# Moving the low weights of a split-precision decoder block by 128 bytes in their buffers

## The chip, the cores and the metric

The kernel runs on one core of a Trainium2 chip. Its time is the device time of one execution in microseconds. Before the change it is 522.29 us, the median of 3 runs (522.06 to 523.15). Five engines work side by side, each through its own list of instructions: TensorE (PE, with its weight loads shown apart as PEld), VectorE (DVE), ScalarE (ACT), GpSimd (POOL) and SyncE (SP), whose queue issues nearly all transfers.

## The reference, cut to what matters

One decoder block of width 1024 over 256 tokens: a normalised input, three token mixers side by side (a sparse attention, an mLSTM and attention to a fixed memory), gated and merged, then a SwiGLU channel mixer.

```python
h = rmsnorm(x, g_pre_mix);  z = h @ w_in            # queries, keys, gates, ...
y = gm0 * (y_nsa @ w_proj_nsa) + gm1 * (y_ml @ w_proj_ml) + gm2 * (y_mem @ w_proj_mem)
x = x + rmsnorm(y @ w_out, g_post_mix)
gate, up = rmsnorm(x, g_pre_ffn) @ w_ffn_in          # 1024 x 5632
x = x + rmsnorm((silu(gate) * up) @ w_ffn_down, g_post_ffn)
```

All is float32, and nearly all of the work is matrix products with weights that are read once.

## The kernel before, in words

**Split precision.** TensorE takes float32 in a rounded form ("float32r") at one pass. To keep the precision, each operand is split in two: a high part, the operand rounded by a copy on ScalarE, and a low part, the operand less its high part, by a subtraction on VectorE (`split`, lines 970 to 973). A product of two operands then takes three matmuls (`mm3`, line 1005): high weights with high input, high weights with low input, low weights with high input. This document calls these three a triplet.

**Units.** Weights come in 161 units of 128 x 1024 numbers (512 KB), each by one transfer into one of four `raw` buffers (`fetch`, line 979). From there the split writes `whi` and `wlo`, of which there are four buffers each (`room` at line 990, `parts` at 995, `unit` at 1000). A buffer of these two is 1088 numbers wide, 64 more than a unit, so that a unit can stand further in. Where it stands is the argument `shift`, counted in numbers of 4 bytes, one for the high and one for the low part.

**Two ways to use a unit.** In `fmaj` (line 1010, called through `fpair`, line 1018, and in the projections at line 1696) the weights are held in TensorE, 128 x 128 at a time, and 256 columns of input (the 256 tokens) stream past them. A unit is 8 such blocks, so 8 triplets, 24 matmuls with 24 weight loads; the high block is loaded for each of its two matmuls. These calls take the default shift. In `tmaj` (line 1025) and in the class `Blocks` (line 1054) it is the other way round: activations are held and 512 columns of weights stream. These calls pass their own shift, 48 or 0. The memory's keys (line 1192) use `room()` with the default shift and hold weights over 256 columns too. The four first units of the FFN's gate and up rows are written into buffers of their own (`wq`, line 1775), which the default does not reach.

**Addresses.** `lay_out` (line 880) gives each buffer a fixed place. A table (`RESIDUE`, line 877) sets at which remainder of 256 bytes it begins. `whi`, `wlo`, `raw` and the buffers tagged G, C, V and qs begin at 0; those tagged KK, E, Y and hh, among them the inputs of `fmaj`, begin at 192. A `whi` or `wlo` buffer is 4352 bytes long, 17 times 256, so all four begin at remainder 0, and each block of 128 columns (512 bytes) does as well. The weights of the gates (`gw`, line 1292) stand 32 numbers, 128 bytes, into a `whi` buffer. A shift of 48 numbers is 192 bytes.

**Order.** Every operation is first recorded (`Plan.record`, line 196) and then issued by a planner (`schedule`, line 369) from modelled costs, due times and a written table of corrections (`EARLY`, line 547). Costs depend on engine, kind and size of an operation, not on addresses. All instructions are issued by the planner at line 917, which is therefore the line of every row in the profile; rows are told apart by the names of tiles. `hh` is the normalised input of the mixers, `xc` that of the FFN, `u` the FFN's hidden values; `pd`, `pss`, `pt` and `pv` are tiles of the accumulator.

**Stages** (us from the span's start): the memory's keys and values and the input projections up to about 270, with attention and mLSTM among them; the three output projections to 308; the output product to about 322; the first part of the FFN input, with products saved by sums of row blocks, to 360; the rest of the FFN input, `block` by `block` (line 1804, 2 units each), to 453; the FFN's down product to the end.

Of the kernel before, what the change touches and what calls it, by code (L numbers as in the profile page):

```python
# [920 lines left out]
def block_kernel(ctx, tc, order, xN, xT, memN, head, cst, vec, row, wg, w1, w2, W, out):  # L921
# [48 lines left out]
    def split(hi, lo, src):  # L970
        op = ACT.activation(hi, src, AF.Copy)
        DVE.tensor_sub(lo, src, hi.bitcast(F32))
        return op
# [5 lines left out]
    def fetch(key):  # L979
        if key in ahead:  # L980
            if not room4:
                room4.append(bigt("KK", 1, [P, len(ahead), 1024], F32, "rawx"))
            raw = ready[key] = room4[0][:, ahead.index(key), :]
        else:
            raw = ready[key] = wpool.tile([P, 1024], F32, tag="raw", bufs=4, name="raw")
        dma(out=raw, in_=W[len(order)])
        order.append(key)
        return raw

    def room(shift=(0, 0)):  # L990


        return [wpool.tile([P, 1088], F32R, tag=t, bufs=4, name=t)[:, n:n + 1024] for t, n in zip(("whi", "wlo"), shift)]

    def parts(raw, into=None, shift=(0, 0)):
        hi, lo = into or room(shift)
        split(hi, lo, raw)
        return hi, lo

    def unit(key, into=None, shift=(0, 0)):  # L1000
        if key not in ready:
            fetch(key)
        return parts(ready.pop(key), into, shift)
# [14 lines left out]
    def fpair(xs, w, i, ps_new=ps_d):  # L1018

        ps = ps_new([P, 2, S])  # L1020
        for j in range(2):
            fmaj(ps[:, j, :], xs, range(KD), unit((w, 2 * i + j)))
        return ps

    def tmaj(xs, *key, n=4, ps_new=ps_d, into=None, last=0, shift=lambda u: 48):


        ps = [ps_new([P, 512]) for _ in range(2)]

        def use(u, tb, wu):  # L1030
            hi, lo = wu
            for kk in range(2):
                k = 2 * u + kk
                t = slice(tb * P, (tb + 1) * P)
                w = slice(kk * 512, (kk + 1) * 512)
                PE.matmul(ps[tb], xs[0][:, k, t], hi[:, w], start=(k == 0), stop=False)
                PE.matmul(ps[tb], xs[0][:, k, t], lo[:, w], start=False, stop=False)
                PE.matmul(ps[tb], xs[1][:, k, t], hi[:, w], start=False, stop=(k == 2 * n - 1))

        for u in range(n - last):  # L1040
            w = unit((*key, u), shift=(shift(u),) * 2)
            for tb in range(2):
                use(u, tb, w)
        us = range(n - last, n)
        ws = [unit((*key, u), into and into[u], (shift(u),) * 2) for u in us]
        for tb in range(2):
            for u, w in zip(us, ws):
                use(u, tb, w)
        return ps
# [4 lines left out]
    class Blocks:  # L1054
# [30 lines left out]
        def seven(self, n, u):  # L1085

            k, first, last = 2 * u, n == 0, n == len(self.sums) - 1
            both = self.both.pop(u, None) or self.pair(u)
            raw, dif = self.shift(u), (48, 48)
            s = [[self.sums[n][:, x, i] for x in range(2)] for i in range(4)]  # L1090
            w0 = parts(both[:, 0].rearrange("p k n -> p (k n)"), shift=raw)
            w1 = room(dif)
            split(w1[0][:, H1], w1[1][:, H1], both[:, 1, 1])
            self.three(self.m1, self.held(k, 0), w0, H0, first, last)
            self.into(0, 0, self.held(k + 1, 0), w0, H1)
            self.into(1, 0, s[3], w1, H1)
            t = work.tile([P, 1024], F32, tag="p", bufs=2, name="dif")
            DVE.tensor_sub(t.rearrange("p (k n) -> p k n", k=2), both[:, 1], both[:, :, 0])
            w = parts(t, shift=dif)
            self.three(self.m5, s[0], w, H0, first, last)  # L1100
            self.three(self.m7, s[2], w, H1, first, last)
            t2 = work.tile([P, 1024], F32, tag="p", bufs=2, name="dif")
            DVE.tensor_add(t2[:, H0], t[:, H1], both[:, 0, 0])
            DVE.tensor_sub(t2[:, H1], both[:, 0, 1], t2[:, H0])
            w = parts(t2, shift=raw)
            self.three(self.m6, s[1], w, H0, first, last)
            self.into(0, 1, self.held(k + 1, 1), w, H1)
# [84 lines left out]
    for u in range(4):  # L1192
        if u and ("mem_k", u) not in ready:
            fetch(("mem_k", u))
        raw = ready.pop(("mem_k", u)) if u else mt[:, 264:1288]
        w = room()
        pieces = HEAD[u]
        for h in range(2):
            if h < pieces:
                c = slice(1024 // pieces * h, 1024 // pieces * (h + 1))  # L1200
                split(w[0][:, c], w[1][:, c], raw[:, c])
            mem_in(2 * u + h)
        for k in (2 * u, 2 * u + 1):
            b = lambda j: slice(512 * (k % 2) + P * j, 512 * (k % 2) + P * j + P)
            for i, (x, y) in enumerate(((w[0], mh), (w[0], ml), (w[1], mh))):
                for j in range(4):
                    PE.matmul(kps[j // 2][:, j % 2, :], x[:, b(j)], y[:, k, :],
                              start=k == 0 and i == 0 and j % 2 == 0, stop=k == KD - 1 and i == 2 and j % 2 == 1,
                              skip_group_check=True)
# [806 lines left out]
```

## Time and profile before

| what | before |
|---|---|
| median of 3 runs | 522.29 us |
| the profiled execution | 523.74 us |
| its span, first to last instruction | 521.7 us |
| granted TensorE clock, mean | 0.996 |
| TensorE busy | 513.6 us, 98% of the span, 3778 matmuls |
| its weight loads | 484.7 us, 93% |
| VectorE / ScalarE busy | 435.1 us (83%) / 360.0 us (69%) |
| GpSimd busy | 6.8 us (1%) |
| DMA | 97.18 MB, mean 186 GB/s |

The profile is that of one execution. A row of a group names line, engine, operation, `out<-in` by the program's tiles, sizes, the count, the busy time in us, the mean length of one in ns, and the idle time before them with what ended it. Matmuls overlap: the length of one is longer than the step from one start to the next, and it is the step that counts for the time. A row of a stretch gives its length, then for each engine the busy time and in brackets the number of instructions that touch it (TensorE, its weight loads, VectorE, ScalarE, GpSimd), then the granted clock, the DMA share and GB/s. A row of the timeline gives the start in us, the length in us, and how many instructions of one kind were merged in it.

### The profile page before, as it was taken

To read this page: it belongs to the slowest core of one execution; us is meant where nothing else is said; L and a number is where in the kernel's file an instruction comes from. 1 tells how busy PE (TensorE), PEld (TensorE's weight loads), DVE (VectorE), ACT (ScalarE), POOL (GpSimd) and SP (SyncE) were. 2 spreads that over 40 slices of the span, in tenths; PEclk is the share of its full clock that TensorE was granted. 3 is DMA by queue.
4 is the path that set the end of the run, shared out by engine and by line. 5 is a ranking of instruction groups with operands and counts; after the bars stand their busy time and mean duration, and the time that the engine had idled before them with its cause. 6 is when DMAs were issued, how large, how long until landed. Compare 5 with 4: busy or idle time off the path is not lost.

```text
span 521.7 us, 10043 instructions
## 1 busy us (share of the span) xinstructions
PE 513.6 (98%) x3778; PEld 484.7 (93%) x3778; DVE 435.1 (83%) x902; ACT 360.0 (69%) x723; POOL 6.8 (1%) x20
## 2 busy tenths in 40 slices
PE   8999999999999999999999999999999999999995
PEld 8899998989899999999999998888999999988884
DVE  5699898798989998987888868789976568798983
ACT  6787897577799887977996437748454456566641
POOL 0000000000000100000000000100000000000000
PEclk9999999999999999999999999999999999999998
DMA  8987547635343273254485653734656555463422
GB/s 310 394 340 272 183 148 210 208 122 201 122 146 138 86 279 122 82 202 162 165 296 198 232 173 131 281 144 163 228 174 202 171 193 171 154 215 108 138 106 80
DMA packets 28560, 97.18 MB, mean 186 GB/s; under 512 B 3296, under 2 KB 5216, under 8 KB 28256
## 3 DMA queue, kind: packets, MB, share of 16 engines
q1 hardware_dynamic: 28368, 96.29, 53.4%
q8 instruction: 29, 0.48, 0.4%
q10 hardware_dynamic: 144, 0.26, 0.1%
q14 instruction: 19, 0.16, 0.1%
HBM read 94.44 MB, written 1.05 MB: 183 GB/s over the span
## 4 chain that ended last, share of the span: by engine, by line
PE 94%; DMA 3%; DVE 1%; ACT 1%; SPq 0%; issue 0%; DVEq 0%
PE pd L917 51%; PE pss L917 28%; PE pvn L917 3%; PE pt L917 2%; PE sc L917 2%; PE ptn L917 2%; DMA xt<-in_xT 2%; DMA raw<-in_W 1%; PE pv L917 1%; DVE wlo L917 1%; PE ph L917 1%; PE ptx L917 1%; PE psm L917 1%; PE pvm L917 1%; PE pn L917 0%; PE pq L917 0%
## 5 line engine op out<-in xcount | busy, mean ns | idle before, releaser
L917 ACT ACTIVATE whi<-raw 128x1024 fp32r<-128x1024 f32 (+1 forms) x146 | 151.6, 1050 | 78.8 <-PE pd L917 39.1
L917 DVE TENSOR_TENSOR wlo<-raw,whi 128x1024 fp32r<-128x1024 f32 (+1 forms) x146 | 174.3, 1205 | 31.3 <-ACT whi L917 28.7
L917 PE MATMUL pd<-hh,whi 128*128 128x256 f32 x800 | 147.0, 280 | 0.0
L917 PEld LDWEIGHTS pd<-hh,whi 128*128 128x128 f32 x800 | 123.6, 188 | 0.2
L917 PE MATMUL pd<-hh,wlo 128*128 128x256 f32 x400 | 111.8, 280 | 0.0
L917 PEld LDWEIGHTS pd<-hh,wlo 128*128 128x128 f32 x400 | 75.3, 188 | 0.1
L917 PE MATMUL pss<-xc,whi 128*128 128x256 f32 x384 | 70.0, 281 | 0.0
L917 PEld LDWEIGHTS pss<-xc,whi 128*128 128x128 f32 x384 | 59.7, 189 | 0.6
L917 PE MATMUL pss<-xc,wlo 128*128 128x256 f32 x192 | 52.9, 281 | 0.0
L917 PEld LDWEIGHTS pss<-xc,wlo 128*128 128x128 f32 x192 | 35.9, 189 | 0.3
L917 PE MATMUL pd<-xc,whi 128*128 128x256 f32 x192 | 35.2, 282 | 0.0
L917 DVE CUSTOM_DVE_ANT_0 sc<-sc,msk 128x16 f32<-128x16 f32 (+2 forms) x96 | 27.2, 313 | 6.0 <-PE sc L917 3.8
L917 PE MATMUL pd<-whi,hh 128*128 128x512 f32 x96 | 31.6, 397 | 0.0
L917 PEld LDWEIGHTS pd<-xc,whi 128*128 128x128 f32 x192 | 29.7, 189 | 0.0
L917 ACT ACTIVATE pp<-sc,mx 128x128 f32<-128x128 f32 (+1 forms) x64 | 26.8, 432 | 0.5 <-DVE mx L917 0.4
L917 PE MATMUL pd<-xc,wlo 128*128 128x256 f32 x96 | 26.6, 281 | 0.0
L917 PE MATMUL pd<-whi,u 128*128 128x512 f32 x72 | 24.1, 392 | 0.0
L917 ACT ACTIVATE whi<-dif 128x1024 fp32r<-128x1024 f32 x12 | 12.6, 1056 | 13.3 <-PE pd L917 7.4
L917 PEld LDWEIGHTS pd<-whi,hh 128*128 128x128 f32 x96 | 17.9, 188 | 3.2
L917 PE MATMUL pd<-wlo,hh 128*128 128x512 f32 x48 | 19.0, 396 | 0.0
L917 DVE TENSOR_TENSOR wlo<-dif,whi 128x1024 fp32r<-128x1024 f32 x12 | 14.6, 1223 | 5.2 <-ACT whi L917 5.1
L917 PE MATMUL pss<-whi,u 128*128 128x512 f32 x56 | 18.7, 390 | 0.0
(392 smaller groups left out, 1134.1 us busy)
## 6 DMA issues: line engine op xcount, KB each, us to landing
raw<-in_W SPq DMA_DIRECT2D x145, 512.0 KB, 4.1
raws<-in_W SPq DMA_DIRECT2D x12, 512.0 KB, 4.6
w<-in_w SPq DMA_DIRECT2D x2, 1024.0 KB, 7.8
rawx<-in_W SPq DMA_DIRECT2D x4, 512.0 KB, 5.5
xn<-in_xN SPq DMA_DIRECT2D x2, 512.0 KB, 9.8
mn<-in_memN SPq DMA_DIRECT2D x2, 512.0 KB, 7.5
xt<-in_xT SPq DMA_DIRECT2D x2, 512.0 KB, 8.4
kk<-kk SPq DMA_DIRECT2D x8, 128.0 KB, 3.1
```

The lines of the kernel that those rows point to most:

```text
L917: op.ins_ = getattr(op.real, op.method)(*map(arg, op.a), **{k: arg(x) for k, x in op.kw.items()})
```

## The change

The default of `shift` goes from (0, 0) to (0, 32) in `room`, `parts` and `unit`. Where no shift is passed, the low part of a unit therefore begins 32 numbers, 128 bytes, further in its buffer, at remainder 128 of 256 bytes instead of 0. The high part stays at 0. VectorE writes the low part there and TensorE loads it from there. Calls that pass a shift, and units written into buffers of their own, are untouched. Instructions, their order and their waits stay the same.

```diff
-    def room(shift=(0, 0)):
+    def room(shift=(0, 32)):
         return [wpool.tile([P, 1088], F32R, tag=t, bufs=4, name=t)[:, n:n + 1024] for t, n in zip(("whi", "wlo"), shift)]
 
-    def parts(raw, into=None, shift=(0, 0)):
+    def parts(raw, into=None, shift=(0, 32)):
         hi, lo = into or room(shift)
         split(hi, lo, raw)
         return hi, lo
 
-    def unit(key, into=None, shift=(0, 0)):
+    def unit(key, into=None, shift=(0, 32)):
         if key not in ready:
             fetch(key)
         return parts(ready.pop(key), into, shift)
```

## The prediction

> **What bounds the kernel now.** I read the page first, then the waits of TensorE, then stretches of time side by side, and last the timeline where a pace changes. The page, with its matmul groups:
>
> ```profile
> PE 513.6 (98%) x3778; PEld 484.7 (93%) x3778; DVE 435.1 (83%) x902; ACT 360.0 (69%) x723; POOL 6.8 (1%) x20
> ...
> PE 94%; DMA 3%; DVE 1%; ACT 1%; SPq 0%; issue 0%; DVEq 0%
> ...
> L917 PE MATMUL pd<-hh,whi 128*128 128x256 f32 x800 | 147.0, 280 | 0.0
> ...
> L917 PE MATMUL pd<-hh,wlo 128*128 128x256 f32 x400 | 111.8, 280 | 0.0
> ...
> L917 PE MATMUL pss<-xc,whi 128*128 128x256 f32 x384 | 70.0, 281 | 0.0
> ...
> L917 PE MATMUL pss<-xc,wlo 128*128 128x256 f32 x192 | 52.9, 281 | 0.0
> ...
> L917 PE MATMUL pd<-xc,whi 128*128 128x256 f32 x192 | 35.2, 282 | 0.0
> ...
> L917 PE MATMUL pd<-xc,wlo 128*128 128x256 f32 x96 | 26.6, 281 | 0.0
> ```
>
> TensorE is busy for 98% of the span and makes 94% of the chain. These six groups (2064 matmuls) are most of those that hold weights for 256 columns. The waits of TensorE, all of them:
>
> ```profile
> PE warm L917 <- POOL mhalf L917: 1.0, 1, 1.0
> PE pd L917 <- ACT whi L917: 0.7, 1, 0.7
> ```
>
> So after the start TensorE waits for nobody. Its time can change only through the pace at which matmuls follow each other. That pace is not one number. Seven stretches that hold little but matmuls over 256 columns; the first count in brackets is the number of matmuls that touch the stretch:
>
> ```profile
> 36.00:40.00 4.00, 4.00 (x36) 4.00 (x35) 3.93 (x9) 3.92 (x8) 0.00 (x0) 1.00 1.02 410
> 44.00:48.00 4.00, 4.00 (x38) 4.00 (x37) 3.91 (x9) 2.85 (x5) 0.00 (x0) 1.00 1.03 411
> 193.00:198.00 5.00, 5.00 (x45) 5.00 (x44) 4.19 (x11) 4.43 (x12) 0.00 (x0) 1.00 0.31 106
> 222.00:229.00 7.00, 7.00 (x64) 7.00 (x63) 6.57 (x17) 4.71 (x12) 0.00 (x0) 1.00 0.65 219
> 272.00:302.00 30.00, 30.00 (x267) 30.00 (x267) 25.18 (x31) 18.13 (x21) 0.00 (x0) 1.00 0.64 226
> 377.00:407.00 30.00, 30.00 (x257) 30.00 (x256) 19.78 (x28) 13.73 (x21) 0.00 (x0) 1.00 0.58 191
> 407.00:437.00 30.00, 30.00 (x257) 30.00 (x256) 20.99 (x35) 16.50 (x24) 0.00 (x0) 1.00 0.51 172
> ```
>
> and one group from the fifth and one from the sixth stretch:
>
> ```profile
> L917 PE MATMUL pss<-ynh,wlo 128*128 128x256 f32 x32 | 8.8, 276 | 0.0
> ```
> ```profile
> L917 PE MATMUL pss<-xc,wlo 128*128 128x256 f32 x43 | 11.7, 281 | 0.0
> ```
>
> A matmul touches a stretch if it starts in it or up to its own length before it, so the step is (stretch + length) / count: (30 + 0.276)/267 = 113.4 ns in the projections and (30 + 0.281)/257 = 117.8 ns in the FFN input. Same shape, same granted clock of 1.00: a quick and a slow pace, 4.4 ns apart. Traffic does not explain it: 36 to 40 us (118.9 ns) and 44 to 48 us (112.5 ns) move the same 410 GB/s with DVE equally full. The timeline shows where it turns:
>
> ```profile
> 374.00 0.28 PE L917 MATMUL pd<-xc,wlo 128*128 128x256 f32 x1
> ...
> 374.34 0.28 PE L917 MATMUL pd<-xc,wlo 128*128 128x256 f32 x1
> ...
> 374.68 0.28 PE L917 MATMUL pd<-xc,wlo 128*128 128x256 f32 x1
> ...
> 374.91 0.60 PE L917 MATMUL ptu<-cs,ut 128*128 128x128 f32 x4
> ...
> 375.46 0.28 PE L917 MATMUL pd<-xc,wlo 128*128 128x256 f32 x1
> ...
> 375.82 0.28 PE L917 MATMUL pd<-xc,wlo 128*128 128x256 f32 x1
> ...
> 376.17 0.28 PE L917 MATMUL pd<-xc,wlo 128*128 128x256 f32 x1
> ```
>
> A triplet (high weights with high input, high with low, low with high) takes 0.34 us before four transposes and 0.353 us after them (0.71 for two), and from there the slow pace holds to 437 us at least. So the pace is a state: something foreign to the run sets it, and an unbroken run keeps it. I read it as two regular streams of reads, input and next weights, which either mesh or keep bumping into each other; the profile shows the two paces, not their cause.
>
> **The change part by part.** No instruction, wait, transfer or queue position is added, removed or moved, and the planner's costs do not look at addresses. What moves is the start of `wlo` in its buffer: 128 bytes on, for the units taken with the default shift. By the code these are 108 units of 24 matmuls (mem_k 4, kv 8, qk_ml 8, q_mem 4, q_nsa 8, g_merge 24, projections 16, ffn_in 36): 2592 matmuls, a third of which (864) load low weights.
>
> *DVE's write of the low part.* The nearest rows are the same subtraction written to places 0 and 192 past a multiple of 256 bytes (400 to 440 us, 308 to 318 us):
>
> ```profile
> L917 DVE TENSOR_TENSOR wlo<-raw,whi 128x1024 fp32r<-128x1024 f32 x14 | 17.0, 1224 | 12.6 <-ACT whi L917 12.6
> ```
> ```profile
> L917 DVE TENSOR_TENSOR wlo<-raw,whi 128x1024 fp32r<-128x1024 f32 x3 | 3.7, 1221 | 0.1
> ```
>
> Three ns apart, and TensorE does not wait for DVE: nothing either way. Were that cover gone, 3 ns on 108 writes would be 0.3 us. ACT writes the high part where it did.
>
> *The load of low weights beside the stream of the low input.* The input starts 192 past a multiple of 256 bytes, all weights at 0; now every third load starts at 128, and the next goes back to 0. No row shows just this. Two come near. First, the compressor's two chains of 16 (input at 0, stationary at 192, the same distance as 192 and 128):
>
> ```profile
> 52.26 2.05 PE L917 MATMUL ph<-w1s,st 128*128 128x256 f32 x16
> 54.14 0.41 PE L917 MATMUL pd<-hh,whi 128*128 128x256 f32 x2
> ```
> ```profile
> 56.99 1.98 PE L917 MATMUL ph<-w1s,st 128*128 128x256 f32 x16
> 58.81 0.33 PE L917 MATMUL phT<-w2t,hs 128*128 128x64 f32 x2
> ```
>
> 1.88/16 = 117.5 ns and 1.82/16 = 113.8 ns: the new distance, held throughout, also has both paces. So the distance alone sets nothing; what is new is that it jumps twice in each triplet. Second, the gates' weights, which stand at 128 while the same input streams at 192, over 512 columns, against the quiet end of the kernel:
>
> ```profile
> 40.96 0.86 PE L917 MATMUL pgf<-hh,gw 128*128 128x512 f32 x3
> 41.67 0.28 PE L917 MATMUL pd<-hh,whi 128*128 128x256 f32 x1
> ...
> 41.90 1.32 PE L917 MATMUL pgf<-hh,gw 128*128 128x512 f32 x5
> 43.06 0.40 PE L917 MATMUL pd<-hh,whi 128*128 128x256 f32 x2
> ```
> ```profile
> 498.53 0.39 PE L917 MATMUL pd<-wlo,u 128*128 128x512 f32 x1
> ...
> 499.21 0.39 PE L917 MATMUL pd<-wlo,u 128*128 128x512 f32 x1
> ```
>
> 0.71/3 = 237 and 1.16/5 = 232 ns against 0.68/3 = 226.7: 5 to 10 ns more. But the stretch before them was at the slow pace (36 to 40 us) and the stretch behind them at the quick one (44 to 48 us): the jump of distance went with a change to the quick pace. From these rows a low load lies between -4.4 ns, with its two neighbours gaining as much, and +10 ns.
>
> I take the gain as likeliest: a slow pace lives on regular repetition, and a jump twice per triplet breaks it within a few steps, while a state in which reads miss each other is less in need of it. The stock of slow steps: in the FFN input some 800 of 864 at 4.4 ns, 3.5 us (its groups' means are 281 to 282 ns, a fast stretch like the one before 374.9 us is the exception); in the projections' 384 nearly none (272 to 302 us); in the remaining 1344 about half by the four short stretches (two slow, two fast), 3.0 us, with bounds 0 and 5.9. Together 6.5 us. Other work still cuts in, each cut is a new entry, and a slow pace needs some steps to break, so I take two thirds: **-4.3 us**. On the profiled execution, 523.74 us with its span of 521.70, that gives 519.4. The median of the runs is 1.45 us lower, 518.0 on its base. If that 1.45 us is itself slow stock (the run of 272 to 302 us alone, 265 steps, would be worth 1.2 us if it were slow), the median's stock is 5.05, two thirds are 3.4, and 518.9 results. I forecast **518.4 us**. Room for it is there: at 407 to 437 us DVE is at 70%, ACT at 55% and DMA at 51%, and a pace 4% quicker leaves all under 75%; what is late next is nothing.
>
> **Rivals.** *The low load collides (slower).* Loading low weights at 128 while the low input streams costs more than it now does, in each triplet, as at the gates' weights. For it: their 5 to 10 ns, in all eight. Against it: few samples, a longer stream, and a quick pace behind them. With 864 low loads at 5 to 10 ns, less the 4.4 that about half already pay, it is 2.6 to 6.7 us slower; with a middle of 4, **526.3 us**. It decides when a low load adds over 5 ns while the rest turns fast (4.3/864), or over 1.2 ns while the rest stays (1.04/864).
>
> *The entries are only drawn anew.* Both states survive the jumps, but each run enters at another phase. The run from 375 to 437 us and on may turn fast (62/0.1178 = 526 steps or more, -2.3 us), the one from 272 to 302 us slow (265 steps, +1.2), and the early ones cancel. For it: four transposes are enough to turn a run. It gives 520.0 to 523.5, and half way to the first **521.2 us**.
>
> *The address does nothing.* The pace is set at entry by something that does not see where weights lie; the two compressor chains, one distance and two paces, speak for it. Then **522.3 us**. The Trainium skill, "TensorE: Matmul & The Clock Gate", Part 2 ("Step-by-step: what each phase is for"), says that TensorE has two independent read ports into SBUF, so that loading the next weights takes nothing from the running matmul; by that rule the sum is zero and this rival holds. The trace does not refute it, but two paces at clock 1.00 without a wait are nothing it foresees.
>
> **How the numbers follow.** Forecast 0.48; collision 0.22; entries drawn anew 0.18; nothing 0.12. What a measurement can tell from no change is 0.2%, 1.04 us: faster is below 521.25. The forecast lies there wholly, and of the redraw, whose middle stands at that edge, 0.10; the redraw gives 0.05 to the same and 0.03 to slower. Faster 0.48 + 0.10 = 0.58; same 0.12 + 0.05 = 0.17; slower 0.22 + 0.03 = 0.25. The forecast's own range is 516.2 (all 6.5 less a few entries, off the median) to 520.6 (a quarter of the stock). The range reaches into the collision to its middle, 516.2 to 526.0.
>
> **What would show it.** Right: stretches of pure FFN input hold about 267 matmuls in 30 us instead of 257, with 276 ns each instead of 281, and the run behind the transposes at 375 us is fast or turns fast within a few triplets. Collision: triplets of over 0.353 us, the third step the long one. Redraw: long runs of both paces, in other places. Nothing: the same stretches, the same counts. Counts unchanged and time lower, or a new wait on TensorE, would make my account wrong.

## The result, and the profile after

The changed kernel takes 519.25 us (median of 5 runs, 517.58 to 519.31) against 523.03 us of the kernel before in the same session (5 runs, 522.06 to 523.56): a ratio of 0.9925 with a 95% interval of 0.9906 to 0.9944, 3.8 us less. The profiled execution took 519.27 us with a span of 516.7, against 523.74 and 521.7: 4.5 us less in time, 5.0 in span. The forecast was 518.4 us, and -4.3 us on the profiled execution. In what follows, one of the 12 executions of the kernel with both operands moved took 1840.86 us and is left out of its ratio.

The page of the kernel after, its engines, the chain by engine and the six groups of matmuls over 256 columns:

```profile
PE 508.7 (98%) x3778; PEld 479.9 (93%) x3778; DVE 434.8 (84%) x902; ACT 360.2 (70%) x723; POOL 6.8 (1%) x20
...
PE 94%; DMA 3%; DVE 1%; ACT 1%; SPq 0%; issue 0%; DVEq 0%
...
L917 DVE TENSOR_TENSOR wlo<-raw,whi 128x1024 fp32r<-128x1024 f32 (+1 forms) x146 | 174.4, 1206 | 29.3 <-ACT whi L917 28.1
L917 PE MATMUL pd<-hh,whi 128*128 128x256 f32 x800 | 146.2, 279 | 0.0
...
L917 PE MATMUL pd<-hh,wlo 128*128 128x256 f32 x400 | 111.4, 279 | 0.0
...
L917 PE MATMUL pss<-xc,whi 128*128 128x256 f32 x384 | 67.9, 276 | 0.0
...
L917 PE MATMUL pss<-xc,wlo 128*128 128x256 f32 x192 | 52.1, 276 | 0.0
...
L917 PE MATMUL pd<-xc,whi 128*128 128x256 f32 x192 | 34.1, 277 | 0.0
...
L917 PE MATMUL pd<-xc,wlo 128*128 128x256 f32 x96 | 26.1, 276 | 0.0
```

The shares are nearly the same, the counts the same. TensorE's busy time went from 513.6 to 508.7 us, which is nearly the whole difference of the spans. The four groups that read the FFN input `xc` went from 281 and 282 ns to 276 and 277, the two that read `hh` only from 280 to 279. All waits of TensorE in the kernel after:

```profile
PE warm L917 <- POOL mhalf L917: 1.0, 1, 1.0
PE pd L917 <- ACT whi L917: 0.4, 1, 0.4
PE pss L917 <- DVE wlo L917: 0.3, 2, 0.2
```

1.7 us in all, as before. The seven stretches of the prediction, in the kernel after:

```profile
36.00:40.00 4.00, 4.00 (x38) 4.00 (x37) 3.93 (x8) 3.93 (x7) 0.00 (x0) 1.00 1.04 417
44.00:48.00 4.00, 4.00 (x38) 4.00 (x37) 3.91 (x9) 2.32 (x4) 0.00 (x0) 1.00 1.02 409
193.00:198.00 5.00, 5.00 (x46) 5.00 (x45) 4.24 (x12) 4.62 (x12) 0.00 (x0) 1.00 0.38 111
222.00:229.00 7.00, 7.00 (x64) 7.00 (x63) 6.11 (x18) 4.41 (x11) 0.00 (x0) 1.00 0.61 205
272.00:302.00 30.00, 30.00 (x267) 30.00 (x267) 25.72 (x32) 17.61 (x20) 0.00 (x0) 1.00 0.61 213
377.00:407.00 30.00, 30.00 (x268) 30.00 (x266) 19.66 (x28) 14.63 (x21) 0.00 (x0) 1.00 0.53 176
407.00:437.00 30.00, 30.00 (x267) 30.00 (x266) 23.15 (x42) 17.01 (x27) 0.00 (x0) 1.00 0.61 202
```

Both long stretches of the FFN input hold 267 or 268 matmuls instead of 257. By the prediction's own arithmetic a step there takes (30 + 0.276)/267 = 113.4 ns instead of 117.8. The projections (272 to 302 us) were at 267 and stayed there. The timeline of the kernel after at the four transposes that had turned the pace (they start at 372.88 us here, at 374.91 before):

```profile
372.88 0.60 PE L917 MATMUL ptu<-cs,ut 128*128 128x128 f32 x4
...
373.44 0.28 PE L917 MATMUL pd<-xc,wlo 128*128 128x256 f32 x1
...
373.79 0.28 PE L917 MATMUL pd<-xc,wlo 128*128 128x256 f32 x1
...
374.13 0.28 PE L917 MATMUL pd<-xc,wlo 128*128 128x256 f32 x1
...
374.47 0.28 PE L917 MATMUL pd<-xc,wlo 128*128 128x256 f32 x1
```

From low load to low load 0.35, 0.34 and 0.34 us: the first triplet after the transposes is slow, the next are quick. Before the change the same place led into over 60 us at the slow pace.

The packed traces hold the start of every matmul, so the steps can also be read one by one: from the start of a matmul that holds weights over 256 columns to the start of the next, if that is one too. Steps over 135 ns, which are interruptions, are left out. Before the change nearly all of these steps lie near 113 or near 118 ns; those of 116 ns or more are counted here as slow. A run is a series of such steps without another instruction or an interruption between them; there are 102. "The rest" are the memory's keys and values and the input projections.

| steps of 116 ns or more | before | after |
|---|---|---|
| FFN input | 791 of 845 | 28 of 845 |
| output projections | 47 of 371 | 9 of 371 |
| the rest | 527 of 1223 | 235 of 1220 |
| among the first twelve of each run | 395 of 808 | 271 of 808 |
| among all later ones | 970 of 1631 | 1 of 1628 |

The last two rows show what the change does. A run can still start at the slow pace after an interruption, but from its thirteenth step on it is quick, in every stage. The kernels with part of the change, below, agree: with the FFN input alone moved, 0 of its 747 later steps are slow, and with everything else moved 0 of 580 in the rest.

### The profile page after: what moved, and what is told of

Same layout as the page of the kernel before. It is cut to its first block, busy times and chain, and to the rows that moved or that the text cites. A ratio compares the mean times of both kernels' runs of the same rounds, so it can differ in the third digit from the quotient of the medians.

```text
span 516.7 us, 10043 instructions
## 1 busy us (share of the span) xinstructions
PE 508.7 (98%) x3778; PEld 479.9 (93%) x3778; DVE 434.8 (84%) x902; ACT 360.2 (70%) x723; POOL 6.8 (1%) x20
## 4 chain that ended last, share of the span: by engine, by line
PE 94%; DMA 3%; DVE 1%; ACT 1%; SPq 0%; issue 0%; DVEq 0%
PE pd L917 51%; PE pss L917 28%; PE pvn L917 3%; PE pt L917 2%; PE sc L917 2%; PE ptn L917 2%; DMA xt<-in_xT 2%; DMA raw<-in_W 1%; PE pv L917 1%; DVE wlo L917 1%; PE ph L917 1%; PE ptx L917 1%; PE psm L917 1%; PE pvm L917 1%; PE pq L917 1%; PE pn L917 0%
## 5 line engine op out<-in xcount | busy, mean ns | idle before, releaser
L917 ACT ACTIVATE whi<-raw 128x1024 fp32r<-128x1024 f32 (+1 forms) x146 | 151.6, 1050 | 74.6 <-PE pd L917 36.3
L917 DVE TENSOR_TENSOR wlo<-raw,whi 128x1024 fp32r<-128x1024 f32 (+1 forms) x146 | 174.4, 1206 | 29.3 <-ACT whi L917 28.1
L917 PE MATMUL pss<-xc,whi 128*128 128x256 f32 x384 | 67.9, 276 | 0.0
L917 PE MATMUL pd<-xc,whi 128*128 128x256 f32 x192 | 34.1, 277 | 0.0
```

What stands on the lines that cost most here:

```text
L917: op.ins_ = getattr(op.real, op.method)(*map(arg, op.a), **{k: arg(x) for k, x in op.kw.items()})
```

## The experiments

All of them are moves of addresses, and in the traces the order of instructions on each engine is the changed kernel's in each. The diffs are against the kernel before unless they say otherwise, and each ratio is to the kernel before as it ran beside (medians of 522.62 to 523.09 us). "Counts" are the matmuls in 272 to 302, 377 to 407 and 407 to 437 us (where a fence has no row for the last, it is as in the one before it): 267 or 268 is the quick pace, 256 to 258 a mean step like that of the slow pace. Before: 267, 257, 257. After: 267, 268, 267.

### Both parts moved: place without a jump

```diff
-    def room(shift=(0, 0)):        # and parts, unit
+    def room(shift=(32, 32)):
```

> High and low weights both stand 128 bytes in; nothing jumps within a triplet. Theory J (the jump of remainder between the loads of a triplet breaks the slow pace): the slow pace can live again, so long stretches at 117.8 ns come back; if the FFN input is entered as before, 30 us of it from 377 us hold about 257 matmuls and the time is 522 to 523.5 us; 267 matmuls there would need another entry. Rival P (the place 128 of the low weights is itself better than 0): no slow stretches, 267 matmuls, 519 us. Rival R (any new addresses only draw the entries anew): some stretches of each pace, 519 to 523.5 us.

Measured: 525.27 us, ratio 1.0046 (1.0034 to 1.0058).

```profile
272.00:302.00 30.00, 30.00 (x267) 30.00 (x267) 24.89 (x31) 18.39 (x23) 0.00 (x0) 1.00 0.63 226
377.00:407.00 30.00, 30.00 (x257) 30.00 (x256) 20.56 (x30) 13.78 (x20) 0.00 (x0) 1.00 0.55 183
407.00:437.00 30.00, 30.00 (x257) 30.00 (x256) 20.16 (x35) 15.74 (x23) 0.00 (x0) 1.00 0.51 171
```

All weights now stand where only the low ones stand in the changed kernel, and the long runs are what they were before: one quick, two slow. So the place 128 has no merit of its own for them; the low weights have to stand apart from the high ones. Most of its 2.7 us are lost in the early stages: in the rest, 988 of 1225 steps are slow, against 527 of 1223 before, which is 2.0 us. A stretch that was quick before (first row) has become slow (second row, with both parts moved):

```profile
43.50:48.00 4.50, 4.50 (x42) 4.50 (x41) 4.41 (x10) 3.34 (x6) 0.00 (x0) 1.00 1.02 394
```
```profile
43.50:48.00 4.50, 4.50 (x40) 4.50 (x39) 4.41 (x10) 2.48 (x5) 0.00 (x0) 1.00 0.98 394
```

### The low part 256 bytes further

```diff
-    def room(shift=(0, 0)):        # and parts, unit
+    def room(shift=(0, 64)):
```

> Low weights stand 256 bytes in, remainder 0 again, but at another address. Theory J with a period of 256 bytes: as the kernel before, long slow stretches, 257 matmuls in 30 us of FFN input, 522 to 523.5 us. Rival P2 (distance between the high and the low part counts, whatever the remainder) : 267 matmuls, 519 us. Rival R: some stretches of each pace, not the same ones as before.

Measured: 522.36 us, ratio 1.0003 (0.9992 to 1.0013).

```profile
272.00:302.00 30.00, 30.00 (x267) 30.00 (x266) 25.72 (x32) 17.57 (x20) 0.00 (x0) 1.00 0.60 209
377.00:407.00 30.00, 30.00 (x257) 30.00 (x256) 18.77 (x27) 13.90 (x20) 0.00 (x0) 1.00 0.56 181
```

Twice the move and no effect: for the low weights it is the remainder of 256 bytes that counts, as far as one such move can show it. The long runs also have their old paces, which speaks against entries that are drawn anew by any touch.

### The low part 64, 192 or 96 bytes further

```diff
-    def room(shift=(0, 0)):        # and parts, unit
+    def room(shift=(0, 16)):       # 64 bytes; (0, 48): 192; (0, 24): 96
```

> Low weights stand 64 bytes in: a jump of half the size. Theory J: any jump breaks the slow pace, 267 matmuls in 30 us of FFN input, 518 to 520 us. Rival P (place 128): slow stretches stay, 257 matmuls, 522 to 523.5 us. If only half a period of 256 bytes works, this stands with the kernel before or between.

> Low weights stand 192 bytes in, the remainder of the input itself: a jump of 64 bytes the other way. Theory J: 267 matmuls in 30 us of FFN input, 518 to 520 us. Rival P (place 128): slow stretches stay, 257 matmuls, 522 to 523.5 us. Rival C (weights at the remainder of the input they are loaded beside collide): over 117.8 ns per step, slower than 523.5 us.

> As the change, but the low weights stand 96 bytes further instead of 128, between the 64 that kept only the slow pace (528.5 us, 256 matmuls in 377 to 407 us) and the 128 of the change. If only the half period itself does it: 528 us and 256 or 257. If a jump near the half is enough: 519.2 us and 267. Between: both paces possible, 521 to 524 us.

Measured: 528.52 us with 64 bytes, ratio 1.0111 (1.0098 to 1.0124); 527.92 us with 192, ratio 1.0103 (1.0089 to 1.0118); 527.67 us with 96, ratio 1.0095 (1.0078 to 1.0111). With 64 bytes:

```profile
272.00:302.00 30.00, 30.00 (x256) 30.00 (x255) 24.18 (x31) 19.03 (x25) 0.00 (x0) 1.00 0.63 218
377.00:407.00 30.00, 30.00 (x256) 30.00 (x255) 22.48 (x34) 15.01 (x24) 0.00 (x0) 1.00 0.57 181
```

and with 96:

```profile
272.00:302.00 30.00, 30.00 (x258) 30.00 (x257) 24.42 (x31) 19.21 (x25) 0.00 (x0) 1.00 0.64 220
377.00:407.00 30.00, 30.00 (x257) 30.00 (x256) 22.52 (x34) 15.08 (x24) 0.00 (x0) 1.00 0.57 181
```

(192 bytes: 257, 257, 257.) By their counts the three look alike: the projections, quick in the kernel before, are slow, and no long run is at the quick pace. But the counts are means, and they hide that the pace is not the slow pace of the kernel before, in which the steps are 118 ns at every place. Mean steps in 377 to 437 us, in ns, by their place in the triplet (1: from high weights with high input to high with low; 2: on to low with high; 3: on to the next triplet). The load of the low weights starts 3 to 4 ns after the matmul of the second step, which streams the low input:

| low weights at (high at 0) | 1 | 2 | 3 |
|---|---|---|---|
| 0, before | 117.7 | 117.9 | 117.8 |
| 64 | 119.0 | 119.4 | 116.3 |
| 96 | 114.9 | 122.7 | 116.3 |
| 128, after | 113.3 | 113.2 | 113.5 |
| 192 | 118.1 | 118.2 | 117.6 |

At 64 bytes the single steps vary from 112 to 124 ns; at 96 it is one long step in each triplet. That falsifies the reading that any jump leaves the quick pace, on which the prediction rests; of the five moves tried, one helps, three harm and one is neutral. A quarter of the period in either direction harms, and 96 bytes, three quarters of the way to the change, harm as much.

### The mirror image: the high part moved

```diff
-    def room(shift=(0, 0)):        # and parts, unit
+    def room(shift=(32, 0)):
```

> The mirror image of the change: the high weights stand 128 bytes into their buffers, the low ones at 0, so the stream of weights makes the same two jumps of half a period in each triplet. Theory H (after the four runs before): a jump of 128 bytes in a period of 256 leaves only the quick pace, whichever part jumps. Then as the changed kernel: 519.2 us, ratio 0.990 to 0.995, 267 matmuls in 377 to 407 us. Rival P (it is the place 128 of the low load beside the low input at 192 that helps): now the high weights stand at 128 and the low ones at 0 as before, so two loads of three are at the new place and beside another input; 257 matmuls and 522 us or more.

Measured: 520.35 us, ratio 0.995 (0.9938 to 0.9963).

```profile
32.00:39.50 7.50, 7.50 (x65) 7.50 (x65) 7.43 (x12) 6.60 (x12) 0.00 (x0) 1.00 0.89 347
43.50:48.00 4.50, 4.50 (x40) 4.50 (x39) 4.41 (x9) 2.41 (x5) 0.00 (x0) 1.00 0.96 388
...
272.00:302.00 30.00, 30.00 (x267) 30.00 (x266) 25.25 (x31) 18.03 (x20) 0.00 (x0) 1.00 0.65 225
377.00:407.00 30.00, 30.00 (x267) 30.00 (x266) 19.72 (x29) 14.41 (x21) 0.00 (x0) 1.00 0.59 192
```

The long runs are as in the changed kernel, so there the jump of half a period counts and not which part makes it. The first two stretches, in the kernel after:

```profile
32.00:39.50 7.50, 7.50 (x68) 7.50 (x67) 7.43 (x14) 6.79 (x12) 0.00 (x0) 1.00 0.88 343
43.50:48.00 4.50, 4.50 (x42) 4.50 (x42) 4.41 (x9) 2.80 (x5) 0.00 (x0) 1.00 1.01 405
```

(7.5 + 0.28)/65 = 119.7 and (4.5 + 0.28)/40 = 119.5 ns with the high part moved, 114.4 and 113.8 ns after the change. With high weights at 128 these stretches are slow in spite of the jump, the second of them although it was quick in the kernel before (42). Step by step, after the twelfth of each run, 339 of the 583 steps of the rest are slow, and 20 of the 1050 of projections and FFN input. So half a period isn't the whole rule, and why the early stages differ isn't settled.

### The change in the FFN input alone, and everywhere else

```diff
-        fmaj(ps[:, j, :], xs, range(KD), unit((w, 2 * i + j)))
+        fmaj(ps[:, j, :], xs, range(KD), unit((w, 2 * i + j), shift=(0, 32 * (w == "ffn_in"))))
```

The second kernel is the changed one with `w != "ffn_in"` in this place.

> The low weights are moved by 128 bytes in the FFN input's 36 units alone. By the stock of the prediction: its 864 matmuls lose 4.4 ns on some 750 of them, -3.3 us, so 519.3 us and a ratio of 0.9935 to 0.995; 267 matmuls in 377 to 407 and 407 to 437 us, and the early stretches as before the change (36, 38, 45, 64). If the gain came from the earlier stages: 522 us and 257.

> The low weights are moved by 128 bytes everywhere but in the FFN input. By the prediction the rest holds 3.0 us of slow steps, bounds 0 and 5.9, two thirds of it recovered: -2.0 us, 520.6 us. By the sum of the measured -3.4 to -3.8 us with the FFN's -3.3 us only -0.1 to -0.5 us remain: 522.1 us, ratio 0.998 to 1.000. 257 matmuls in 377 to 437 us either way, early stretches 38, 38, 46, 64.

Measured: in the FFN input alone 519.42 us, ratio 0.9935 (0.9922 to 0.9949); everywhere else 521.51 us, ratio 0.9979 (0.9967 to 0.9991), both beside 522.71 us before. In the FFN input alone:

```profile
272.00:302.00 30.00, 30.00 (x267) 30.00 (x266) 25.68 (x33) 17.57 (x20) 0.00 (x0) 1.00 0.60 214
377.00:407.00 30.00, 30.00 (x267) 30.00 (x266) 19.66 (x28) 14.70 (x21) 0.00 (x0) 1.00 0.55 179
```

Everywhere else (the projections again at 267):

```profile
377.00:407.00 30.00, 30.00 (x257) 30.00 (x256) 18.91 (x26) 13.56 (x20) 0.00 (x0) 1.00 0.57 176
```

-3.3 us from the FFN input, as expected to the tenth, and -1.2 us from everything else, between the two sums expected. Together -4.5 us, against -3.8 us (0.9906 to 0.9944, which is 2.9 to 4.9 us) for the whole change: they add up within what the runs can tell.

### The other operand moved as well, or alone

The FFN input's low part `xl` stands 128 bytes further, once with the change (the diff is against the kernel after) and once with the kernel before. The rows of `xc` become 2304 bytes long, nine times 256, so that all other remainders stay:

```diff
-    xc = bigt("KK", 1, [P, KD, 2, S], F32R, "xc")
-    xh, xl = xc[:, :, 0], xc[:, :, 1]
+    xc = bigt("KK", 1, [P, KD, 576], F32R, "xc")
+    xh, xl = xc[:, :, 0:S], xc[:, :, S + 32:2 * S + 32]
```

> The change, and beside it the FFN input's low part xl also stands 128 bytes further in its buffer, so that in the FFN input the streamed operand jumps by 128 bytes too (on the high-weight, low-input step). Theory M (what counts is how the two streams stand to each other): the jumps of the stream now change the relation that the weights' jump made; 257 matmuls in 377 to 437 us can come back, 522 us, or more. Theory W (what counts is the sequence of the weights' own places): 267 matmuls and 519.2 us as the changed kernel. The early stages are the changed kernel's under both.

> All weights stand as before the change; only the FFN input's low part xl stands 128 bytes further, so the streamed operand makes two jumps of half a period per triplet and the weights none. Counted as distance between input and the weights loaded beside it, the three steps of a triplet are 192, 64, 192 bytes, as in the changed kernel. Theory D (that distance is all that counts): 267 matmuls in 377 to 407 us and 519.4 us, as with the change in the FFN input alone. Theory S (a jump of the streamed operand costs by itself, a jump of the weights helps): 252 matmuls or fewer, as in the run before with both jumps, and 523 to 525 us. D has against it that the run before, with 192 in all three steps as before the change, had 252 and not 257.

Measured: with the change 523.65 us, ratio 1.0018 (1.0007 to 1.0029); alone 523.6 us, ratio 1.0003 (0.9995 to 1.0012). With the change:

```profile
272.00:302.00 30.00, 30.00 (x267) 30.00 (x266) 25.86 (x32) 16.63 (x19) 0.00 (x0) 1.00 0.61 208
377.00:407.00 30.00, 30.00 (x252) 30.00 (x251) 18.34 (x26) 13.27 (x19) 0.00 (x0) 1.00 0.52 176
407.00:437.00 30.00, 30.00 (x252) 30.00 (x252) 21.47 (x36) 15.99 (x23) 0.00 (x0) 1.00 0.52 176
```

and alone:

```profile
272.00:302.00 30.00, 29.25 (x258) 29.05 (x257) 24.73 (x31) 17.20 (x20) 0.00 (x0) 1.00 0.59 207
377.00:407.00 30.00, 30.00 (x257) 30.00 (x256) 20.11 (x29) 13.77 (x20) 0.00 (x0) 1.00 0.57 186
```

The 258 in the projections of the second is no slow pace: TensorE waited 0.75 us there, once in this execution, and 51 of 369 steps are slow, against 47 of 371 before. With the change, only the place of the streamed input differs from the kernel after, and the FFN input goes from 113.4 to a mean of (30 + 0.28)/252 = 120.2 ns a step, slower than before the change. By their place in the triplet the steps are 118.9, 122.2 and 119.6 ns, with single ones from 112 to 130; with `xl` alone moved 117.2, 119.1 and 117.0. So it is no matter of the weights alone: how the streamed operand stands counts too (theory M, against W). But a simple distance isn't it: with both moved, the distance is 192 in all three steps as in the kernel before, and the pace is another; with `xl` alone it is 192, 64, 192 as in the changed kernel, and 257 came, not 267. Theory D fails in both runs. S fails by its count, 252 or fewer, though 523.6 us lies in its range: the jump of the input alone costs nothing beyond the mean of the slow pace. No rule that was put forward predicts all of these counts.

### The stages that stream 512 columns

Two additions to the changed kernel, diffs against it: the low weights that are streamed jump by half a period, and in the other kernel the low hidden values that are held in the down product do.

```diff
-            w = unit((*key, u), shift=(shift(u),) * 2)
+            w = unit((*key, u), shift=(shift(u), shift(u) - 32))
...
-        ws = [unit((*key, u), into and into[u], (shift(u),) * 2) for u in us]
+        ws = [unit((*key, u), into and into[u], (shift(u), shift(u) - 32)) for u in us]
```

```diff
-    us = [bigt(tg, n, [P, 2, 4, S], F32R, f"u{i}") for i, (tg, n) in enumerate(tags)]
+    us = [bigt(tg, n, [P, 2080], F32R, f"u{i}") for i, (tg, n) in enumerate(tags)]
+    us = [[t[:, a:a + 1024].rearrange("p (k s) -> p k s", k=4) for a in (0, 1056)] for t in us]
```

> The change, and beside it the low weights that are streamed over 512 columns (the units taken with a shift of 48 numbers: q of both attentions, memory scores, output) stand at 16 numbers, 128 bytes nearer, so that the streamed operand jumps there while the stationary one does not. 288 matmuls. Theory S (a jump of the streamed operand costs): 2.4 ns or more on each, +0.7 us or more over the changed kernel's 519.25. Theory W2 (a jump in either stream breaks a slow pace, steps of 228 to 236 ns become 226.7): about 3 ns on each, -0.9 us, 518.4 us.

> The change, and beside it the low part of the hidden values stands 128 bytes further in its buffer. In the down product these are stationary and the weights stream over 512 columns, so the loaded operand jumps by half a period twice per triplet, as in the change, in a stage that the change leaves alone (some 470 matmuls). The changed kernel has 88 and 89 matmuls in 460 to 480 and 480 to 500 us, so (20 + 0.391)/88 = 231.7 and 229.1 ns a step, against 226.7 at its quiet end. If the change's gain carries over to 512 columns: 90 in each, 3 to 4 ns on 400 steps, -1.4 us, 517.9 us. If these 3 to 5 ns are something else (cuts by other work, traffic): 88 to 89 and 519.2 us.

Measured: 519.13 us, ratio 0.9913 (0.9899 to 0.9926), and 519.02 us, ratio 0.9916 (0.9902 to 0.993). Both intervals overlap with that of the change itself (0.9906 to 0.9944), so the times don't tell the three kernels apart. The traces do. Mean steps over 512 columns, read one by one as above:

| streamed and held | kernel after | streamed low weights moved | held low hidden values moved |
|---|---|---|---|
| weights, `hh` held (115 steps) | 228.9 ns | 231.4 ns | 228.9 ns |
| weights, `yh` held (91) | 227.8 ns | 230.1 ns | 227.8 ns |
| weights, `u` held (200) | 228.5 ns | 228.6 ns | 231.6 ns |

Each move lengthens the steps that it touches, by 2.3 to 3.1 ns, and leaves the others alone: some 0.5 us in the first kernel, 0.6 in the second. For the first that is the 2.4 ns of theory S, and W2 fails; in the second a cost stands where a gain was expected. The groups' means move the same way, here with `u` held in the kernel after and, below it, with its low part moved:

```profile
L917 PE MATMUL pd<-whi,u 128*128 128x512 f32 x72 | 24.1, 391 | 0.0
```
```profile
L917 PE MATMUL pd<-whi,u 128*128 128x512 f32 x72 | 24.3, 394 | 0.0
```

The counts, 88 and 89 in 460 to 480 and 480 to 500 us in the kernel after and 88 and 88 with the low part moved, are too coarse for this: one matmul in 88 is 2.6 ns a step. What holds these steps above 226.7 ns without a move stays open.

## Why the prediction was right, and where it was not

**What bounds the kernel.** Right. TensorE's busy time fell by 4.9 us and the span by 5.0, its waits stayed at 1.7 us, and no other engine came into the chain. VectorE is busy for 77% of 407 to 437 us now, a little over the 75% foreseen, and TensorE waits for it 0.3 us in all.

**DVE's write insensitive.** Right: the group's mean is 1206 ns, and was 1205; in 390 to 440 us, where only moved writes stand, their median is 1225 ns, and was 1224.

**Two paces, kept by an unbroken run.** Right for the kernel before: the quick steps have a mean of 113.4 ns and the slow steps one of 117.9, and from the thirteenth step of a run on 727 of the FFN input's 747 are slow and 10 of the projections' 303. It is no rule for other addresses: with the low weights at 64 or 96, or `xl` moved, the steps within a triplet are uneven, and counts of 256 to 258 are only their mean.

**The new distance by itself sets nothing; what is new is the jump.** The first half is right: both parts at 128 kept both paces in the long runs, though more of the early steps became slow. The second half is right for this jump. The FFN input turned to the quick pace one triplet after its entry, and the projections kept it.

**"A jump twice per triplet breaks it within a few steps, while a state in which reads miss each other is less in need of it."** This step failed as a rule. For the 128 bytes of the change it is right to the letter: 1 of 1628 steps after the twelfth of a run is slow. Jumps of 64, 96 and 192 bytes leave no long run quick, and cost 4.6 to 5.9 us by the medians. A jump of 128 does what the step said when the low weights make it; made by the high ones, it leaves the early stages slow. So the sign of the forecast rested on an argument that holds for one jump in four. Nothing in the profile before distinguishes 64 from 128 bytes, so that the change was the one that helps was luck as far as that profile goes; the chance of 0.22 for the collision was what covered this. That rival's price, 2.6 to 6.7 us (by its own terms the lower end is 2.4), is what the other jumps cost. At 96 bytes its mechanism is seen too: the step that streams the low input and loads the low weights takes 122.7 ns, the other two 114.9 and 116.3. At 64 and 192 bytes no single step carries the cost.

**The stock of slow steps.** Its size was about right. Over a quick step of 113.4 ns, the profiled execution before holds 3.5 us of slow steps in the FFN input, 0.2 in the projections and 2.4 in the rest; the sum had 3.5, nearly none and 3.0. The change takes 3.4, 0.2 and 1.1 us of it, 4.7 in all, against the forecast's 4.3. So the two thirds stand for two very different shares, nearly all of the FFN input and under half of the rest. The reason given for them, that each cut is a new entry and a slow pace needs some steps to break, fits the difference: the first twelve steps of a run, of which 271 of 808 stay slow, are 98 of 845 in the FFN input and 637 of some 1220 in the rest. The runs with part of the change agree: 3.3 us for the FFN input alone, 1.2 us for everything else. Three other kernels that leave the early stages as before (256 bytes, the FFN input alone, `xl` alone) have 387 to 404 slow steps in the rest, so the profiled execution holds more of them than its sisters.

**The number.** The forecast of 518.4 us is 0.85 us under the median. Most of that is the base: the forecast was worked out from 522.29 us, the median of 3 runs, and the 5 runs beside the result have 523.03. Counted from base to base it is -3.9 us against -3.8.

**The rivals.** "The address does nothing" is refuted: an FFN input moved alone, with nothing else touched, is 3.3 us faster, and moves of 64 bytes are 1.1% slower. The Trainium skill, "TensorE: Matmul & The Clock Gate", Part 2 ("Step-by-step: what each phase is for"), has two independent read ports, so that loading the next weights takes nothing from the running matmul. This case's runs don't agree with that to the last 4 to 6%: at the same clock of 1.00 the mean step goes from 113.4 to 117.8 and 120.2 ns with the remainders of the two operands. Whether the ports, the buffers' rows or something behind them meet isn't shown. "The entries are only drawn anew" is refuted for the long runs by the paces that stayed (256 bytes further) and by the ones that all turned the same way (the others); what is left of it is the first dozen steps of each run.

**Still open.** Which relation of the two operands' remainders gives which pace; why high weights at 128 leave the early stages slow, and what ends a slow entry after a dozen steps with the low ones there; whether the quick pace is possible at all with `xl` moved alone. No run separates these.

## What to carry to other kernels

Where TensorE waits for nobody and yet the same matmul at the same clock shows two step lengths in different stretches, look at where its two operands stand modulo 256 bytes, and try moves of the loaded part against the other by half that period. Don't infer one such move from another: 64, 96 and 192 bytes cost 1% here, 128 gained 0.75% and 256 did nothing, and over 512 columns moves of 128 bytes lengthened the steps by 1%. Size the gain by the slow steps that stand deep in unbroken runs, not by all of them: the first dozen after each interruption kept their pace. And read the steps one by one before calling equal means the same pace.

## What the runs showed of the hardware that was not expected

- The pace of the same matmuls depends on both operands' places modulo 256 bytes: low weights 256 bytes further give a ratio of 1.0003, 64 to 192 further 0.9925 to 1.0111, and the streamed `xl` 128 further turns 0.9925 into 1.0018.
- The dependence is not gradual: of the low part's places 0, 64, 96, 128 and 192, with the high part at 0, only 128 gives the quick pace in all the long stretches (267 in 30 us); 0 shows both paces; 64, 96 and 192 show 256 to 258 alone.
- With the low weights at 128 a slow entry ends within twelve steps: of the later steps, 1 of 1628 takes 116 ns or more, against 970 of 1631 before.
- The least favourable of these kernels (528.5 us) and the most favourable (519.0 to 519.3 us) differ by over 9 us, 1.8%, with the same instructions in the same order.
- Equal means hide different patterns: 257 matmuls in 30 us are steps of 118 ns each in the kernel before, and of 115, 123 and 116 ns in turn with the low weights at 96. With both operands jumping, steps of 112 to 130 ns have a mean of 120.2.
- Over 512 columns a jump of 128 bytes in the low part of either operand costs 2.3 to 3.1 ns a step, where over 256 columns one of the held weights' low part takes 4.4 off a slow step.
